# 32-column matmuls in fours over the column quarters, and score pairs over the row halves, in a decoder-layer step

## The chip, the cores and the metric

The kernel runs on one core of a Trainium2 chip. The metric is the time of one execution on the device in microseconds, taken as the median of the runs. The engines are TensorE (PE in the profile; its weight loads are PEld), VectorE (DVE), ScalarE (ACT), GpSimd (POOL) and SyncE (SP), which here only issues transfers.

## What is computed

One layer of a hybrid decoder for two groups with the same weights: a prompt of 1024 tokens, and 8 samples of 4 new tokens each, with 512 past tokens of keys and values in pages of 128. Cut to what the change touches, the reference is:

```python
def diff_attn_core(q, k, v, q_pos, k_pos, lam):
    s = jnp.einsum('bqhid,bkhid->bhiqk', q, k) * (ATTN_HEAD_DIM ** -0.5)   # two maps i, heads h, d = 64
    s = jnp.where(rel >= 0, s + bias, -jnp.inf)
    pr = jax.nn.softmax(s, axis=-1)
    a = pr[:, :, 0] - lam * pr[:, :, 1]
    return jnp.einsum('bhqk,bkhd->bqhd', a, v)                             # v: 128 wide
# prompt: 8 blocks of 128 queries; samples: past_k = cache_k[page_table], 4 heads, 4 pages each
mem_k, mem_v = memory_kv(mem_prompt, p)                                    # the samples have cached ones
s = jnp.einsum('bqhd,bmhd->bhqm', cq, mem_k) * (CA_HEAD_DIM ** -0.5)       # 4 heads of 256, 256 memory tokens
co = jnp.einsum('bhqm,bmhd->bqhd', jax.nn.softmax(s, -1), mem_v)
```

Around it stand an RMS norm and input projection, a diagonal state-space recurrence with its gate, the output projection, and a gated feed-forward of width 2816 with a convolution. All is float32; the large products are made of three matmuls each on a high and a low part (type fp32r).

## The kernel before

The program is one long stream per engine. Stages are written as Python generators that yield costs; `drive` and `par` interleave them by rates and so set the order in which instructions are emitted, and a scheduler then places them engine by engine, by priority and by when their inputs are ready. Each engine runs its own row of instructions strictly in that order. Tiles come from pools with a fixed number of buffers; a tile whose buffer is still in use waits.

In time, the stages are: input projection head by head with the prompt attention of the head before (0 to about 480 us); from about 390 to 646 us the state-space recurrence (`ssm_setup`, `ssm_data`, `ssm_out`), keys and values of the prompt's memory (`memory_kv`) and the samples' attention over their pages; gate and output projection; from 782 us cross-attention (`wq_head`, `ca_head`, `sample_keys`); from 984 us `sample_values` beside the first part of the cross-attention's output projection; from about 1054 us the rest of it and the feed-forward.

Five places matter here.

*Prompt scores* (`attention.score`). For each block of 128 queries and each map i, whose 64 features lie on the lower or upper 64 partitions, chunks of up to 512 keys go through `mm3` (L180 to L182): high x high, low x high, high x low into a tile `S` of one PSUM bank. A DVE reduction adds the bias and keeps the running minimum. The pool `ps_s` has three such tiles; `ps_o` has one bank for the output `ov` of `value`.

*Paged keys* (`sample_attention.keys`). Four samples share a PSUM tile `Sp`, sample b4 in partitions 32 b4 to 32 b4 + 31 (`tile_position=(0, 32 * b4)`). For each sample the four pages are gathered by SP into one of five buffers `pg`, transposed in four (L1381), copied by ACT into `KT`, and after every second page four matmuls of 256 columns (one per head) follow at L1387. All samples' pages go one sample after the other.

*Paged values* (`values`). Sample by sample, page by page: a gather into `pg`, then one matmul of 512 columns (L1433) into the sample's quarter of `Op`; a fifth one takes the new values `vs_`.

*Memory keys* (`sample_keys`). Per head and sample: a load `kt` (three buffers), transposes (L1793), a copy to `KT`, two matmuls of 256 columns into the sample's quarter of `Ssm` (L1799).

*Memory values* (`sample_values`). 32 pieces `vt` of 128 x 512 (seven buffers, loaded by POOL's queue six ahead), each followed by one matmul of 512 columns into a quarter of `Op` (L1870). Of these four places, the first reads:

```python
if pg % 2:
    for h in range(NH):
        nc.tensor.matmul(Sp[rows, 256 * (pg // 2):256 * (pg // 2) + 256], lhsT=Qb[:, h, b, :],
                         rhs=KT[:, h, :], start=h == 0, stop=h == NH - 1,
                         tile_position=(0, 32 * b4))
```

Of the kernel before, what the change touches and what calls it, by code (L numbers as in the profile page):

```python
# [67 lines left out]
def hymba_step(ctx: ExitStack, tc: tile.TileContext, A: dict, O: dict, upto=99, dbg=None):  # L68
# [7 lines left out]
    def par(*streams):  # L76
        # each stream: a generator of costs, its rate, the share it starts behind, its boost
# [109 lines left out]
    class Carve:  # L187
        """Small tiles cut from a few large ones; a tag names one region."""
# [132 lines left out]
    def ssm_params(st, ps):  # L321
# [58 lines left out]
        # cos and sin of the chunk angle times 0..15, and times 0, 16, ..., 112  # L380
# [67 lines left out]
    ps_s = pool(p2, "ps_s", 3, space=PSUM)  # L448
    ps_o = pool(p2, "ps_o", 1, space=PSUM)
# [217 lines left out]
    def attention(h, last):  # L667
# [9 lines left out]
        def score(t):  # L677
# [3 lines left out]
            Pm = []  # L681
# [3 lines left out]
            split(qh, ql, qT[:, 128 * t:128 * t + 128])  # L685
            for i in range(2):
                pr = slice(64 * i, 64 * i + 64)
                P = at.tile([128, SEQ], F32, tag="P", name=f"P{i}", bufs=4)
                init = 3.0e38
                for c0 in range(0, n, 512):  # L690
                    c1 = min(n, c0 + 512)
                    S = ps_s.tile([128, 512], F32, tag="S", name="S")
                    mm3(S[:, :c1 - c0], qh[pr], ql[pr], kh[pr, c0:c1], kl[pr, c0:c1], True, True)
                    b0 = SEQ - n + c0
                    nc.vector.tensor_tensor_reduce(out=P[:, c0:c1], in0=S[:, :c1 - c0], in1=base[:, b0:b0 + c1 - c0],
                                                   scale=-1.0, scalar=init, op0=ALU.add, op1=ALU.min,
                                                   accum_out=mx[:, i:i + 1])
                    init = mx[:, i:i + 1]
                    yield (c1 - c0) * 3 / 2.4
                nc.vector.tensor_scalar(out=mx[:, i:i + 1], in0=mx[:, i:i + 1], scalar1=sl, scalar2=None,  # L700
                                        op0=ALU.mult)
                nc.scalar.activation(out=P[:, :n], in_=P[:, :n], func=AF.Exp, scale=-sl, bias=mx[:, i:i + 1],
                                     accum_out=ssum[:, t, i:i + 1])
                Pm.append(P)
                yield 10
# [23 lines left out]
        def value(t):  # L729
            ov = ps_o.tile([128, 260], F32, tag="ov", name="ov")  # L730
# [375 lines left out]
    # sample group: the recurrence step by step  # L1106
# [77 lines left out]
    # keys and values of the prompt's memory  # L1184
# [78 lines left out]
    # differential attention of the sample group over its pages  # L1263
    sc = {}

    def sample_tables(sa):
# [29 lines left out]
        # columns: the past, new keys for the first four samples, new keys for the last four  # L1296
# [46 lines left out]
    def sample_attention(sa):  # L1343
# [6 lines left out]
        def gather(src, j):  # L1350
            g = sa.tile([128, 512], F32, tag="pg", name="pg", bufs=PGB)
# [17 lines left out]
        def keys(s):  # L1369
            Sp = ps_j.tile([128, PAST], F32, tag="pjb", name="Sp")  # L1370
            Sps.append(Sp)
            for b4 in range(4):
                b = 4 * s + b4
                rows = slice(32 * b4, 32 * b4 + 32)
                for pg in range(NPG):
                    if pg % 2 == 0:
                        KT = sa.tile([128, NH, 256], F32, tag="KT", name="KT", bufs=2)
                    kp_ = gather(kpg, NPG * b + pg)
# [3 lines left out]
                    c = 128 * (pg % 2)  # L1382
                    nc.scalar.copy(KT[:, :, c:c + 128], pt.rearrange("p (h k) -> p h k", h=4))
                    yield 440
                    if pg % 2:
                        for h in range(NH):
                            nc.tensor.matmul(Sp[rows, 256 * (pg // 2):256 * (pg // 2) + 256], lhsT=Qb[:, h, b, :],  # L1387
                                             rhs=KT[:, h, :], start=h == 0, stop=h == NH - 1,
                                             tile_position=(0, 32 * b4))
                        yield 500  # L1390

        def soft(s):
            Sp = Sps[s]
            Pm = sa.tile([128, PAST + NS], F32, tag="Pm", name="Pm")
# [27 lines left out]
        def values(s):  # L1422
# [3 lines left out]
            for b4 in range(4):  # L1426
                b = 4 * s + b4
                for pg in range(NPG + 1):
                    if pg < NPG:
# [681 lines left out]
```

## Time and profile before

| | us |
|---|---|
| median of 3 runs (1910.13 to 1913.94) | 1912.89 |
| span of the profiled execution | 1912.4 |
| TensorE busy in it | 1842.9 (96%) |
| VectorE busy | 1144.4 (60%) |
| ScalarE busy | 623.8 (33%) |
| GpSimd busy | 473.8 (25%) |

The profiled execution's own time is its span, from its first to its last instruction; it lies within 0.5 us of the median. Busy time is the time in which at least one record of an engine runs. Matmuls are pipelined and their records overlap, so what a matmul costs is read from the start of one to the start of the next, or from the length of a group. A line in the profile may be that of a helper: L54 is every DVE and ACT instruction, L180 to L182 every `mm3`. The granted clock (PEclk) is a share of 2.4 GHz.

### The profile page before, as it was taken

The numbers are of one execution on the slowest core, as the hardware profiler recorded it, in microseconds if no ns is written. First come the engines' busy times: TensorE is split into PE (matmuls) and PEld (weight loads), VectorE is DVE, ScalarE is ACT, GpSimd is POOL, SyncE is SP. The second block draws the span as 40 slices with busy tenths as digits, with TensorE's granted clock in tenths as the row PEclk, the third lists the DMA queues.
The fourth block names the chain that finished last, engine by engine and source line by source line (L and its number), as shares of the span: only waits on it lengthen the run. The fifth ranks groups of instructions, "written<-read, shape, count | busy, mean of one in ns | idle before, by whom it ended". The sixth has DMA issues, their size and how long they took to land. (4 is left out here: it accounts for less than half of the span.)

```text
span 1912.4 us, 29088 instructions
## 1 busy us (share of the span) xinstructions
PE 1842.9 (96%) x11105; PEld 1649.2 (86%) x11105; DVE 1144.4 (60%) x2867; ACT 623.8 (33%) x1425; POOL 473.8 (25%) x547
## 2 busy tenths in 40 slices
PE   7899999889899999999989999999999999999998
PEld 6787897767556799888855999999999999999998
DVE  6976448795876554655452665555656646556554
ACT  6654345545243543344441312112102102112112
POOL 4412321360530024100012333223123123223200
PEclk8888998979799999999999999999999999999999
DMA  7202112134355342322243111011111102102102
GB/s 224 68 28 62 44 48 65 48 108 129 113 147 158 117 145 82 95 85 92 78 154 127 56 37 56 27 52 57 45 34 57 55 23 68 45 23 68 45 23 92
DMA packets 160773, 147.15 MB, mean 77 GB/s; under 512 B 14167, under 2 KB 142067, under 8 KB 160634
## 3 DMA queue, kind: packets, MB, share of 16 engines
q1 hardware_dynamic: 135698, 111.03, 19.2%
q0 software_dynamic: 7232, 18.71, 3.2%
q10 hardware_dynamic: 17704, 15.56, 2.4%
q8 instruction: 87, 1.43, 0.3%
q14 instruction: 52, 0.43, 0.1%
HBM read 120.07 MB, written 25.19 MB: 76 GB/s over the span
## 5 line engine op out<-in xcount | busy, mean ns | idle before, releaser
L54 DVE TENSOR_TENSOR xacc<-xacc,pd 128x384 f32<-128x384 f32 (+1 forms) x264 | 134.9, 518 | 168.7 <-PE pd L182 168.7
L54 ACT CAST whi<-raw 128x1024 fp32r<-128x1024 f32 x74 | 77.5, 1049 | 427.9 <-PE pg L181 332.8
L182 PE MATMUL pv<-Xh,wlo 128*128 128x384 f32 (+1 forms) x528 | 171.3, 325 | 0.3 <-DVE wlo L54 0.3
L180 PE MATMUL pv<-Xh,whi 128*128 128x384 f32 (+1 forms) x528 | 171.6, 325 | 0.0
L180 PE MATMUL pd<-ah,dhi 128*128 128x384 f32 (+1 forms) x528 | 171.2, 325 | 0.1
L180 PE MATMUL pg<-Xh,whi 128*128 128x384 f32 (+1 forms) x528 | 171.2, 324 | 0.0
L181 PE MATMUL pv<-Xl,whi 128*128 128x384 f32 (+1 forms) x528 | 171.1, 324 | 0.0
L182 PE MATMUL pd<-ah,dlo 128*128 128x384 f32 (+1 forms) x528 | 170.9, 324 | 0.0
L181 PE MATMUL pd<-al,dhi 128*128 128x384 f32 (+1 forms) x528 | 170.1, 322 | 0.5 <-DVE al L54 0.5
L181 PE MATMUL pg<-Xl,whi 128*128 128x384 f32 (+1 forms) x528 | 170.6, 323 | 0.0
L182 PE MATMUL pg<-Xh,wlo 128*128 128x384 f32 (+1 forms) x528 | 170.2, 322 | 0.0
L54 DVE TENSOR_TENSOR wlo<-raw,whi 128x1024 fp32r<-128x1024 f32 x74 | 107.0, 1448 | 21.1 <-ACT whi L54 20.8
L180 PE MATMUL pp<-Mh,whi 128*128 128x384 f32 (+1 forms) x336 | 109.2, 328 | 0.9 <-ACT Mh L54 0.9
L181 PE MATMUL pp<-Ml,whi 128*128 128x384 f32 (+1 forms) x336 | 108.5, 326 | 0.8 <-DVE Ml L54 0.8
L182 PE MATMUL pp<-Mh,wlo 128*128 128x384 f32 (+1 forms) x336 | 109.2, 327 | 0.0
L798 POOL TENSOR_TENSOR raw<-raw,GT 128x1024 f32<-128x1024 f32 x30 | 67.0, 2233 | 165.2 <-DMA raw<-in_ffn_wg_dram 99.2
L180 PE MATMUL pj<-whi,Xh 128*128 128x384 f32 (+1 forms) x288 | 105.3, 367 | 1.5 <-DVE mx L54 1.5
L181 PE MATMUL pj<-wlo,Xh 128*128 128x384 f32 (+1 forms) x288 | 103.2, 359 | 0.2
L182 PE MATMUL pj<-whi,Xl 128*128 128x384 f32 (+1 forms) x288 | 103.2, 359 | 0.0
L182 PEld LDWEIGHTS pv<-Xh,wlo 128*128 128x128 f32 x528 | 99.7, 189 | 0.5 <-DVE wlo L54 0.4
L181 PEld LDWEIGHTS pd<-al,dhi 128*128 128x128 f32 x528 | 99.2, 188 | 0.8 <-DVE al L54 0.8
L180 PEld LDWEIGHTS pd<-ah,dhi 128*128 128x128 f32 x528 | 99.0, 188 | 0.9 <-ACT ah L54 0.5
(813 smaller groups left out, 4873.8 us busy)
## 6 DMA issues: line engine op xcount, KB each, us to landing
raw<-in_ffn_wg_dram SPq DMA_DIRECT2D x22, 512.0 KB, 3.8
raw<-in_ffn_wv_dram SPq DMA_DIRECT2D x22, 512.0 KB, 3.8
raw<-in_ffn_wd_dram SPq DMA_DIRECT2D x22, 512.0 KB, 3.6
pg<-in_cache_k_dram SPq DMA_DIRECT2D x32, 256.0 KB, 2.7
pg<-in_cache_v_dram SPq DMA_DIRECT2D x32, 256.0 KB, 3.3
kt<-in_cache_mem_k_dram SPq DMA_DIRECT2D x32, 256.0 KB, 2.8
vt<-in_cache_mem_v_dram POOLq DMA_DIRECT2D x32, 256.0 KB, 3.9
raw<-in_w_in_dram SPq DMA_DIRECT2D x48, 128.0 KB, 2.5
```

Source lines behind the costliest of these rows:

```text
L54: return f(*a, **k)
L180: nc.tensor.matmul(out, lhsT=wh, rhs=xh, start=start, stop=False)
L181: nc.tensor.matmul(out, lhsT=wh, rhs=xl, start=False, stop=False)
L182: nc.tensor.matmul(out, lhsT=wl, rhs=xh, start=False, stop=stop)
L798: nc.gpsimd.tensor_tensor(out=raw, in0=raw, in1=g.unsqueeze(2).to_broadcast([128, KD, 128]), op=ALU.mult)
```

## The change

The four 32-column products are reordered so that the matmuls of the four column quarters follow each other (`for b4 in QUADS`, that is 3, 2, 1, 0), under a raised priority that keeps a group together. For this, operands of four samples must be there at once:

- paged keys: page by page over four samples; `KT` holds one page of four samples (8 KB a partition), 16 matmuls of 128 columns follow; page buffers fall from five to two;
- paged values: one tile `V` holds one page of four samples, from four gathers; four matmuls of 512 columns. `KT`, `V` and the probabilities `Pm` share two buffers `big`;
- memory keys: `KT` holds four samples, in one buffer; eight matmuls of 256 columns; loads `kt` have two buffers, `co` two instead of three;
- memory values: 16 pieces of four samples by 256 columns, in three buffers; four matmuls of 256 columns.

The prompt scores take both maps in one tile of two banks, and each of the three matmuls is issued for map 1 and map 0 in turn. `ps_o` is gone: `ps_s` has two tiles of two banks, which also serve the output `ov` and the transposes of x.

```diff
+QUADS = (3, 2, 1, 0)
-    ps_s = pool(p2, "ps_s", 3, space=PSUM)
-    ps_o = pool(p2, "ps_o", 1, space=PSUM)
+    ps_s = pool(p2, "ps_s", 2, space=PSUM)
...
+        pts = ps_s.tile([128, 8, 128], F32, tag="S", name="pt")
         for b in range(2):
-            pt = ps_s.tile([128, 4, 128], F32, tag="S", name="pt")
+            pt = pts[:, 4 * b:4 * b + 4]
...
+                S = ps_s.tile([128, 2, 512], F32, tag="S", name="S")
+                with tc.high_priority():
+                    for j, (q_, k_) in enumerate(((ql, kh), (qh, kl), (qh, kh))):
+                        for i in (1, 0):
+                            pr = slice(64 * i, 64 * i + 64)
+                            nc.tensor.matmul(S[:, i, :w], lhsT=q_[pr], rhs=k_[pr, c0:c1], start=j == 0, stop=j == 2,
+                                             tile_position=(64 * i, 0))
-                    mm3(S[:, :c1 - c0], qh[pr], ql[pr], kh[pr, c0:c1], kl[pr, c0:c1], True, True)
...
-            ov = ps_o.tile([128, 260], F32, tag="ov", name="ov")
+            ov = ps_s.tile([128, 2, 512], F32, tag="S", name="ov")[:, 0]
...
+            for pg in range(NPG):
+                KT = sa.tile([128, 4, NH, 128], F32, tag="big", name="KT", bufs=KTB)
+                for b4 in range(4):
+                    kp_ = gather(kpg, NPG * (4 * s + b4) + pg)
...
+                with tc.high_priority():
+                    for h in range(NH):
+                        for b4 in QUADS:
+                            nc.tensor.matmul(Sp[32 * b4:32 * b4 + 32, 128 * pg:128 * pg + 128],
+                                             lhsT=Qb[:, h, 4 * s + b4, :], rhs=KT[:, b4, h, :],
+                                             start=h == 0, stop=h == NH - 1, tile_position=(0, 32 * b4))
...
+                    V = sa.tile([128, 4, 512], F32, tag="big", name="V", bufs=KTB)
+                    rh = [gather(vpg, NPG * (4 * s + b4) + pg, V[:, b4]) for b4 in range(4)]
...
+                    for b4 in QUADS:
+                        lh = aT[:128 if pg < NPG else NS, pg, 32 * b4:32 * b4 + 32]
+                        nc.tensor.matmul(Op[32 * b4:32 * b4 + 32, :], lhsT=lh, rhs=rh[b4], start=pg == 0,
+                                         stop=pg == NPG, tile_position=(0, 32 * b4))
...
-    PGB = 5
+    PGB, KTB = 2, 2
...
+            for s in range(2):
+                KT = ca.tile([128, 4, 2, NMEM], F32, tag="KT", name="KT", bufs=CKB)
...
+                    for z in range(2):
+                        for b4 in QUADS:
+                            nc.tensor.matmul(Ssm[32 * b4:32 * b4 + 32, :], lhsT=Qc[:, z, 4 * s + b4, :],
...
+                vt = wx.tile([128, 4, 256], F32, tag="vt", name="vt", bufs=3)
...
+                    for b4 in QUADS:
+                        nc.tensor.matmul(Op[32 * b4:32 * b4 + 32, 256 * g:256 * g + 256],
```

(`CKB` is 1.) The scheduler lays out every engine anew. Three places of TensorE's row show what became of it; `pj`, `pp` and `pjm` are projections, `ov` the attention's output, `pt` a transpose, `yp` the recurrence's output.

TensorE, prompt scores of the first heads, before: one map's three matmuls are taken apart, others stand between.

```order
L180 MATMUL ov<-aTh,vh 128x256
L180 MATMUL S<-kh,qh 128x512
L647 MATMUL pt<-ident,qk 128x128 x2
L181 MATMUL S<-kl,qh 128x512
L181 MATMUL ov<-aTl,vh 128x256
```

The same, after: both maps, three times in turn (x2 is map 1 and map 0), in the middle of an output's accumulation.

```order
L181 MATMUL ov<-aTh,vh 128x256
L696 MATMUL S<-kh,ql 128x512 x2
L696 MATMUL S<-kl,qh 128x512 x2
L696 MATMUL S<-kh,qh 128x512 x2
L182 MATMUL ov<-aTl,vh 128x256
```

The six score matmuls moved together; those of the output that stood among them moved behind.

TensorE, the samples' paged values, before: one matmul of one quarter at a time, between the recurrence's matmuls.

```order
L1049 MATMUL yp<-T,Ug 128x128
L1050 MATMUL yp<-CLr,Hr 128x128
L1433 MATMUL Op<-pg,aT 32x512
L965 MATMUL kp<-CLr,Bbr 32x128
L1381 MATMUL pt<-ident,pg 128x128 x4
L1053 MATMUL yp<-CLi,Hi 128x128
L1433 MATMUL Op<-pg,aT 32x512
```

The paged keys near the same place, after: 16 matmuls, four quarters four times, in one piece.

```order
L1054 MATMUL yp<-T,Ug 128x128
L1055 MATMUL yp<-CLr,Hr 128x128
L1058 MATMUL yp<-CLi,Hi 128x128
L1390 MATMUL Sp<-KT,Qb 32x128 x16
L983 MATMUL sp<-ident,T 128x128 x4
```

The paged values stand likewise in ten rows of x4, eight with a page and two with the new values, the keys in eight rows of x16.

TensorE, memory values beside the output projection, before: single matmuls.

```order
L1870 MATMUL Op<-vt,PT 32x512
L182 MATMUL pp<-Mh_11054,wlo 128x384
L180 MATMUL pp<-Mh_11055,whi 128x384
L181 MATMUL pp<-Ml_11058,whi 128x384
L182 MATMUL pp<-Mh_11052,wlo 128x384
L1870 MATMUL Op<-vt,PT 32x512
```

The same, after: fours, with ten to twelve projection matmuls between.

```order
L1882 MATMUL Op<-vt,PT 32x256 x4
L182 MATMUL pp<-col_8554,whi 128x384
L183 MATMUL pp<-coh_8552,wlo 128x384
L182 MATMUL pp<-Ml_11004,whi 128x384
L183 MATMUL pp<-Mh_10998,wlo 128x384
```

Sixteen such fours take the place of the 32 single ones.

## Rows read from the trace of the kernel before

**Rows 1.** Windows: length, busy us (records) of PE, PEld, DVE, ACT, POOL; clock, DMA, GB/s.

```profile
0.00:110.00 110.00, 90.42 (x457) 74.93 (x457) 90.78 (x455) 71.79 (x222) 47.02 (x97) 0.88 0.46 134
110.00:360.00 250.00, 245.71 (x1371) 212.59 (x1371) 149.45 (x553) 121.78 (x397) 52.67 (x76) 0.94 0.16 46
360.00:440.00 80.00, 66.03 (x423) 50.05 (x422) 73.62 (x233) 43.55 (x122) 46.70 (x47) 0.81 0.34 106
440.00:646.00 206.00, 195.67 (x1251) 131.38 (x1250) 135.61 (x320) 79.33 (x150) 46.06 (x40) 0.94 0.45 139
...
782.00:984.00 202.00, 196.60 (x1242) 169.16 (x1240) 108.61 (x434) 88.64 (x213) 5.83 (x6) 0.99 0.26 84
984.00:1054.00 70.00, 67.47 (x244) 34.70 (x245) 20.88 (x44) 14.36 (x32) 21.85 (x37) 0.98 0.49 163
1054.00:1912.00 858.00, 847.81 (x5305) 843.72 (x5305) 490.44 (x678) 147.69 (x180) 217.94 (x214) 1.00 0.16 48
```

**Rows 2.** Windows of L1387 (two), L1433, L1799, L1870 alone, in this order.

```profile
400.00:440.00 40.00, 7.63 (x32) 3.27 (x32) 0.87 0.42 135
440.00:646.00 206.00, 25.90 (x96) 10.59 (x96) 0.94 0.45 139
...
540.00:646.00 106.00, 39.63 (x80) 6.19 (x80) 0.99 0.53 161
...
782.00:984.00 202.00, 32.33 (x128) 11.12 (x128) 0.99 0.26 84
...
984.00:1054.00 70.00, 31.04 (x64) 4.00 (x64) 0.98 0.49 163
```

**Rows 3.** Timeline of TensorE, groups of 32-column matmuls: start, length, line, records.

```profile
1008.95 1.04 PE L1870 MATMUL Op<-vt,PT 128*32 128x512 f32 x2
...
1006.72 1.05 PE L1870 MATMUL Op<-vt,PT 128*32 128x512 f32 x4
...
1014.26 1.06 PE L1870 MATMUL Op<-vt,PT 128*32 128x512 f32 x6
...
820.59 1.05 PE L1799 MATMUL Ssm<-KT,Qc 128*32 128x256 f32 x4
...
429.88 1.91 PE L1387 MATMUL Sp<-KT,Qb 128*32 128x256 f32 x8
```

**Rows 4.** Timeline of TensorE, prompt scores: both maps together, then one alone.

```profile
433.34 0.51 PE L180 MATMUL S<-kh,qh 64*128 64x384 f32 x2
...
433.80 0.52 PE L182 MATMUL S<-kh,ql 64*128 64x384 f32 x2
434.16 0.33 PE L180 MATMUL S<-kh,qh 64*128 64x384 f32 x1
...
434.78 0.66 PE L1381 MATMUL pt<-ident,pg 128*128 128x128 f32 x4
```

**Rows 5.** DMA issues: count, KB each, median us from issue to landing.

```profile
pg<-in_cache_v_dram SPq DMA_DIRECT2D x32, 256.0 KB, 3.3
vt<-in_cache_mem_v_dram POOLq DMA_DIRECT2D x32, 256.0 KB, 3.9
```

**Rows 6.** Waits of POOL: us in total, times, longest.

```profile
POOL vt L1863 <- PE Op L1870: 35.1, 21, 3.6
```

**Rows 7.** Windows of the tile S alone (PE, PEld, DVE, ACT).

```profile
0.00:110.00 110.00, 13.50 (x57) 7.75 (x57) 8.80 (x18) 0.00 (x0) 0.88 0.46 134
...
110.00:360.00 250.00, 44.02 (x160) 23.91 (x159) 32.06 (x55) 0.00 (x0) 0.94 0.16 46
...
360.00:470.00 110.00, 18.61 (x72) 11.44 (x72) 13.39 (x24) 0.00 (x0) 0.86 0.35 109
```

**Rows 8.** Timeline of TensorE: first and last matmul of one attention output.

```profile
442.88 0.38 PE L180 MATMUL ov<-aTh,vh 128*128 128x256 f32 x1 [0.71 <-ACT aTh L54]
...
449.79 0.28 PE L182 MATMUL ov<-aTh,vl 128*128 128x128 f32 x1
```

**Rows 9.** Window of 20 us in which VectorE leads.

```profile
500.00:520.00 20.00, 17.47 (x74) 11.40 (x74) 17.18 (x33) 3.12 (x6) 12.37 (x12) 0.57 0.13 41
```

More of the change, by code (lines that the diff above doesn't have):

```diff
@@ L685, in score @@
             split(qh, ql, qT[:, 128 * t:128 * t + 128])
-            for i in range(2):
[L687 to L692, printed above, removed]
-                    mm3(S[:, :c1 - c0], qh[pr], ql[pr], kh[pr, c0:c1], kl[pr, c0:c1], True, True)
[L694 to L699, printed above, removed]
+            Pm = [at.tile([128, SEQ], F32, tag="P", name=f"P{i}", bufs=4) for i in range(2)]
@@ new lines, in score @@
+            for c0 in range(0, n, 512):
+                c1 = min(n, c0 + 512)
+                w = c1 - c0
+                S = ps_s.tile([128, 2, 512], F32, tag="S", name="S")
[5 more added lines that the diff above has]
+                                             tile_position=(64 * i, 0))
+                yield w * 3 / 2.4
+                b0 = SEQ - n + c0
+                for i in range(2):
+                    nc.vector.tensor_tensor_reduce(out=Pm[i][:, c0:c1], in0=S[:, i, :w], in1=base[:, b0:b0 + w],
+                                                   scale=-1.0, scalar=3.0e38 if c0 == 0 else mx[:, i:i + 1],
+                                                   op0=ALU.add, op1=ALU.min, accum_out=mx[:, i:i + 1])
+                yield w * 3 / 2.4
@@ L1381, in keys @@
                         nc.tensor.transpose(pt[:, 128 * h:128 * h + 128], kp_[:, 128 * h:128 * h + 128], ident)
-                    c = 128 * (pg % 2)
-                    nc.scalar.copy(KT[:, :, c:c + 128], pt.rearrange("p (h k) -> p h k", h=4))
+                    nc.scalar.copy(KT[:, b4], pt.rearrange("p (h k) -> p h k", h=4))
                     yield 440
[L1385 to L1390, printed above, removed]
+                with tc.high_priority():
[4 more added lines that the diff above has]
+                                             start=h == 0, stop=h == NH - 1, tile_position=(0, 32 * b4))
+                yield 1000
         def soft(s):
             Sp = Sps[s]
-            Pm = sa.tile([128, PAST + NS], F32, tag="Pm", name="Pm")
+            Pm = sa.tile([128, PAST + NS], F32, tag="big", name="Pm", bufs=KTB)
             mx = sa.tile([128, 1], F32, tag="mxs", name="mxs")
@@ L1425, in values @@
             Op = ps_x.tile([128, 512], F32, tag="x", name="Op")
[L1426 to L1429, printed above, removed]
[L1430 to L1435 removed]
+            for pg in range(NPG + 1):
+                if pg < NPG:
+                    V = sa.tile([128, 4, 512], F32, tag="big", name="V", bufs=KTB)
+                    rh = [gather(vpg, NPG * (4 * s + b4) + pg, V[:, b4]) for b4 in range(4)]
+                else:
+                    rh = [vs_] * 4
+                yield 10
+                with tc.high_priority():
+                    for b4 in QUADS:
+                        lh = aT[:128 if pg < NPG else NS, pg, 32 * b4:32 * b4 + 32]
+                        nc.tensor.matmul(Op[32 * b4:32 * b4 + 32, :], lhsT=lh, rhs=rh[b4], start=pg == 0,
+                                         stop=pg == NPG, tile_position=(0, 32 * b4))
+                yield 950
             os_ = gp.tile([128, 128], F32, tag="os_", name="os_")
@@ L1777, in ca_head @@
                         continue
[L1778 removed]
+                    co = ca.tile([128, 384], F32, tag="co", name="co", bufs=2)
                     nc.scalar.copy(co[:, :nq], po[:, :nq])
```

79 lines of the change are left out of this document (31 added, 48 removed).

## The prediction

> **What bounds the kernel now.** I read first the busy time of each engine by stage [rows 1]. From 110 us on, TensorE is busy nearly all the time in every stage: 245.7 of 250 us, 195.7 of 206, 196.6 of 202, 67.5 of 70, 847.8 of 858. The exceptions are the first 110 us, where VectorE (DVE) has 90.8 us beside TensorE's 90.4, and 360 to 440 us, where DVE has 73.6 of 80 and TensorE 66.0. So TensorE work that goes is worth most where it is alone at the limit (110 to 360, 782 to 984, 984 to 1054), something where DVE is close behind (440 to 646, 135.6 of 206), and little in the two stretches in which DVE leads. After 1054 us the diff touches nothing.
>
> Next I read what the four groups of 32-column matmuls cost [rows 2]: 33.5 us for the scores against the paged keys (L1387; 7.6 of it ahead of 440 us, 25.9 behind), 39.6 for the paged values (L1433), 32.3 for the memory keys (L1799), 31.0 for the memory values (L1870). Together 136.5 us, 7% of the span, for four small products. The counts are records: each float32 matmul of these lines leaves two.
>
> Then I looked for the thing that the change wants, in the kernel before [rows 3]. Its L1870 matmuls stand in single order among others, but in a few places two or three of different quarters meet. One matmul (2 records) takes 1.04 us, two that meet (4 records) 1.05, three (6 records) 1.06. Four records of one quarter, as in L1799, take 1.05 at half the columns, and eight of one quarter (L1387) 1.91: those follow each other. So matmuls of different column quarters run side by side for 0.01 us each, in this kernel, on this very operation, and those of one quarter do not.
>
> **The change, part by part.** *Sample group.* The work is regrouped, not reduced: 64, 40, 64 and 32 matmuls become 128 of half the columns, 40, 64, and 64 of half the columns, in 8, 10, 8 and 16 groups in which the four quarters alternate. What a group costs is what one quarter's share costs. A paged-key group has per quarter 8 records of 128 columns, as many columns as the x4 row of L1799 at 256: 1.05 us. A paged-value group has 2 records of 512 per quarter: 1.06. A memory-key group has 4 of 256: 1.05 to 1.06. A memory-value group has 2 of 256, half of the 1.06 and no more than all of it: I take 0.6. That is 8 x 1.05 + 10 x 1.06 + 8 x 1.06 + 16 x 0.6 = 8.4 + 10.6 + 8.5 + 9.6 = 37 us for 136.5, so 99 us less TensorE time: 25 at the paged keys, 29 at the values, 24 and 21 at the two memory stages. Four quarters at once are not in these rows (three are). If the fourth had to wait for a second round, each group would cost double, 74 us instead of 37, and the gain would be 62.
> The Trainium skill ("TensorE: Matmul & The Clock Gate", Part 3, Measured speedup vs the span model) speaks against the full figure: it gives 2.38 times for three column tiles and 3.07 for four row tiles. The three-quarter row here gives 3 x 1.04 / 1.06 = 2.94. By the Trainium skill's 3.07 the groups would cost 136.5 / 3.07 = 44 us, an estimate, and the forecast below would be some 5 us later.
>
> *How much of the 99 us reaches the end.* 782 to 984 us: 24 us out of 196.6 busy, DVE at 108.6 and ACT at 88.6 of 202. Nothing else is near its limit, so I take 20. The key tile is now filled for four samples by ACT and has one buffer, and its loads have two instead of three; the 4 us that I leave out are for that. 984 to 1054 us: 21 us out of 67.5. The loads of these values have 0.49 of the DMA engines' time over 70 us; in 49 us the same bytes need 0.70, so they fit, but each lands 3.9 us after its issue [rows 5], and POOL already waits 35.1 us for matmuls to free a buffer [rows 6]. Those waits shrink with the matmuls. From now on three pieces of 512 KB are under way instead of six of 256, so the bytes ahead are the same. POOL issues 16 loads for 32; should each cost four times as much for its four times as many pieces, POOL's 21.9 us in this stage would still be under the 49. I take 16 of 21.
> 440 to 646 us: 19.6 us of the key groups (three quarters of 25.9) and 29 of the values: 48 off 195.7, which leaves 148 against DVE's 135.6. Two engines that both need about 140 of a 158 us stretch do not mesh perfectly, and the new waits are here: two 8 KB buffers serve key tiles, value tiles and probabilities, the page buffers fall from five to two, and a value tile must have all four pages landed (3.3 us from issue to landing [rows 5]) before its group starts. SP issues these pages in order, and behind a page that waits for a buffer stand the memory weights, the recurrence's inputs and its tables. I take two thirds, 32 us. Taken away wholly, this cover costs the 32.
>
> *Prompt scores.* Per chunk, three matmuls of one map and three of the other now alternate between the lower and upper 64 rows. The kernel before has them by accident [rows 4]: three of one map at 384 columns and three of the other at 512 (the x2 rows) run from 433.34 to 434.16, 0.82 us; the three of 384 alone that follow take 434.16 to 434.78, 0.62. Side by side they cost what the longer triple costs. All scores take 13.5 + 44.0 + 18.6 = 76 us of TensorE in the three stretches [rows 7]; halved, 38 saved, less what already pairs. In 0 to 110 and from 360 on DVE sets the pace and I count nothing (at most 7 + 9). In 110 to 360 half is 22 at most; some pairs exist already, and DVE still reads every score. I take 12. The price is the PSUM: three one-bank tiles for scores and one for the output become two tiles of two banks for scores, output and the transposes of x. While an output accumulates, one two-bank tile is left for scores. An output holds its tile long: first matmul at 442.88, last at 449.79 [rows 8]. Bounds for this part: +22 and, with the holds exposed, a loss (last rival).
>
> Sum: 20 + 16 + 32 + 12 = 80 us. The profiled execution's span is 1912.4 us, the median 1912.9, so the two need no correction: **1833 us**.
>
> **Rivals.** *All of it arrives*: 24 + 21 + 48 + 22 and some 5 of the DVE-led stretches, 120 us: about 1793. For it: TensorE is busy above 94% in each of these stages. Against it: the order of each engine is laid out ahead, and DVE is close in 440 to 646.
> *The early part gives nothing*: DVE, POOL and the chain of the recurrence set the length of everything up to 646 us, and only 8 us of the 48 and the two memory stages (36) remain: 1868. For it: DVE at 90.8 of 110 and 73.6 of 80, and from 500 to 520 us DVE is busy 17.2 of 20 while the granted clock is 0.57, mostly the lower of its two levels, 1.2 GHz [rows 9], so TensorE there is not the limit; less work could bring more such stretches. Against it: 245.7 of 250 busy. The Trainium skill names this ("TensorEngine Tiling (Array Packing)", PSUM Bottleneck): tiling speeds up the matmuls, not the emptying of PSUM. The trace agrees so far as the DVE reads of the scores keep their count and size.
> *The shared PSUM tiles turn the sign*: there are 16 outputs in four heads; with 449.79 - 442.88 = 7 us of hold each, 112 us in which the scores have one tile. If the dense matmuls cannot fill it (the second head's memory is freed only when the first head is done), a hold costs up to 6 us, 96 in all, against 68 from the other three terms: 1912 + 96 - 68 = 1940. It decides from 68 / 16 = 4.2 us per output. Against it: TensorE was busy 245.7 of 250 us while the same outputs were held [rows 1], since projections stand between.
> *No side by side at four quarters or for alternated rows*: then only the number of visits falls, and the time is within 4 us of 1912. What meets by accident speaks against it [rows 3, 4].
>
> **How the numbers follow.** Forecast case 0.50 (1812 to 1853); all of it 0.20 (1785 to 1812); early part gives nothing 0.22 (1853 to 1890); turned sign 0.05; no effect 0.03. The range 1793 to 1876 holds the first, some seven tenths of the second and six tenths of the third: 0.50 + 0.15 + 0.14, 0.8. Faster by over 0.2% (about what a measurement of this kernel can tell from no change): 0.92; within: 0.03; slower: 0.05.
>
> **What would show it.** In the profile after: groups of the paged keys at about 1.05 us with 32 records, paged values 1.06 with 8, memory keys 1.06 with 16, memory values about 0.6 with 8, together under 45 us busy instead of 136.5; a triple of score pairs at 512 columns no longer than 0.9 us. The stretch from the first memory query to the end of the memory values, 272 us before, near 236. The time at which the gate's matmuls begin, 646 us before, near 602. Wrong would be: groups at twice these lengths (the fourth quarter waits), TensorE waiting for value pages or for a score tile by tens of us, half-clock stretches beyond those of before, or loads of the memory values landing later than the group that needs them.

## The result, and the profile after

The changed kernel takes 1857.0 us (median of 4 runs, 1851.8 to 1858.4) where the kernel before took 1912.5: a ratio of 0.9711, 95% interval 0.9692 to 0.9730. That is 55 us less, where 80 were forecast (1833 us); the time lies inside the range. The profiled execution has a span of 1854.8 us, 57.6 less than before.

Windows of the kernel after, by its own stages (columns as in [rows 1]: length, busy us of PE, PEld, DVE, ACT, POOL; granted clock, DMA share, GB/s):

```profile
0.00:110.00 110.00, 85.11 (x454) 72.11 (x454) 85.17 (x447) 69.07 (x211) 48.57 (x97) 0.88 0.47 134
110.00:352.00 242.00, 226.94 (x1403) 205.71 (x1403) 156.75 (x577) 125.52 (x421) 54.69 (x77) 0.95 0.17 49
352.00:430.00 78.00, 55.13 (x444) 45.78 (x443) 64.05 (x212) 39.59 (x107) 48.39 (x47) 0.74 0.36 110
430.00:618.00 188.00, 156.26 (x1330) 124.25 (x1328) 148.56 (x343) 81.18 (x157) 45.07 (x39) 0.89 0.51 156
755.00:940.00 185.00, 175.89 (x1227) 164.23 (x1226) 110.06 (x429) 86.87 (x208) 5.37 (x5) 0.96 0.31 93
940.00:994.00 54.00, 49.18 (x316) 35.59 (x315) 23.71 (x49) 15.44 (x36) 16.10 (x20) 0.91 0.69 211
994.00:1854.00 860.00, 850.14 (x5309) 845.75 (x5307) 482.70 (x677) 148.02 (x181) 223.49 (x215) 0.99 0.16 48
```

Against [rows 1] the reader is to see two things. First, TensorE has room in the stages that the change touches: 156 of 188 us where it had been 196 of 206, 49 of 54 where it had been 67 of 70. Second, the clock is lower there: 0.89 for 0.94, 0.96 for 0.99, 0.91 for 0.98. The gate begins at 618 us (646 before), the first memory query is at 755 (782), the last memory-value group ends at 993 (1054). So 28 us were won ahead of the gate, 34 from the first memory query to the end of the memory values (272 to 238), and about 4 were lost elsewhere.

The groups themselves, in the timeline of TensorE after (start, length, line, records; L1390 paged keys, L1439 paged values, L1809 memory keys, L1882 memory values, L696 prompt scores):

```profile
394.27 1.08 PE L1390 MATMUL Sp<-KT,Qb 128*32 128x128 f32 x32
...
543.86 1.07 PE L1439 MATMUL Op<-V,aT 128*32 128x512 f32 x8
...
788.88 1.07 PE L1809 MATMUL Ssm<-KT,Qc 128*32 128x256 f32 x16
...
955.35 0.64 PE L1882 MATMUL Op<-vt,PT 128*32 128x256 f32 x8
...
125.62 0.50 PE L696 MATMUL S<-kh,ql 64*128 64x512 f32 x2
125.96 0.39 PE L696 MATMUL S<-kl,qh 64*128 64x512 f32 x2
126.19 0.39 PE L696 MATMUL S<-kh,qh 64*128 64x512 f32 x2
...
502.19 1.86 PE L1390 MATMUL Sp<-KT,Qb 128*32 128x128 f32 x32
...
603.68 1.93 PE L1439 MATMUL Op<-vs__78,aT 32*32 32x512 f32 x8
```

All four quarters run side by side, at 1.08, 1.07, 1.07 and 0.64 us where 1.05, 1.06, 1.06 and 0.6 were forecast. A pair of score triples at 512 columns takes 0.96 us (125.62 to 126.58), a little over the 0.9 that the prediction named as the limit. The last two rows are groups in stretches at the lower clock.

Groups of instructions of the kernel after, TensorE alone (count, busy us and mean ns, idle time ahead of them and its releaser):

```profile
L1882 PE MATMUL Op<-vt,PT 128*32 128x256 f32 x128 | 10.9, 416 | 2.7 <-DMA vt<-in_cache_mem_v_dram 2.7
L1390 PE MATMUL Sp<-KT,Qb 128*32 128x128 f32 x256 | 9.4, 292 | 1.2 <-ACT KT L55 1.2
L1439 PE MATMUL Op<-V,aT 128*32 128x512 f32 x64 | 8.9, 629 | 2.8 <-DMA V<-in_cache_v_dram 2.8
L1809 PE MATMUL Ssm<-KT,Qc 128*32 128x256 f32 x128 | 8.6, 384 | 2.1 <-ACT KT L55 2.1
L1439 PE MATMUL Op<-vs__78,aT 32*32 32x512 f32 x16 | 3.0, 828 | 0.0
```

Together 40.8 us, for 136.5 in [rows 2]: 96 us less, where 99 were forecast. The waits for loads ahead of these matmuls are 2.7 and 2.8 us, and the transposes ahead of the paged keys (L1384) wait 7.8 us for their pages, 6.1 of it at 412 us. So the work went as forecast; most of what failed to arrive has to be looked for outside these lines.

### The profile page after: what moved, and what is told of

It reads as the page before. It is cut to its first block, busy times and chain, and to the rows that moved or that the text cites. A ratio compares the mean times of both kernels' runs of the same rounds, so it can differ in the third digit from the quotient of the medians.

```text
span 1854.8 us, 29387 instructions
## 1 busy us (share of the span) xinstructions
PE 1732.8 (93%) x11297; PEld 1627.2 (88%) x11297; DVE 1142.1 (62%) x2867; ACT 620.6 (33%) x1425; POOL 477.4 (26%) x531
## 4 chain that ended last, share of the span: by engine, by line
PE 79%; DVE 10%; ACT 3%; DMA 2%; issue 1%; POOL 0%; SPq 0%; ACTq 0%; DVEq 0%; POOLq 0%
PE pp L181 5%; PE pp L182 5%; PE pp L183 5%; PE pv L183 5%; PE pv L181 5%; PE pv L182 5%; PE pd L183 5%; PE pd L182 5%; PE pd L181 5%; PE pg L181 4%; PE pg L182 4%; PE pg L183 4%; PE pj L181 2%; PE pj L182 2%; PE pj L183 2%
## 5 line engine op out<-in xcount | busy, mean ns | idle before, releaser
L181 PEld LDWEIGHTS pv<-Xh,whi 128*128 128x128 f32 x528 | 99.9, 189 | 0.0
```

The source lines that it names most:

```text
L181: nc.tensor.matmul(out, lhsT=wh, rhs=xh, start=start, stop=False)
```

## The experiments

Each row gives the median, the ratio to the kernel before with its 95% interval, and from the timeline of the profiled execution the end of the last attention head (the last matmul that spreads its scale, tile bc), the first matmul of the gate (tile zp), and the time between.

| kernel | us | ratio (interval) | attention ends | gate begins | between |
|---|---|---|---|---|---|
| before | 1912.5 | 1 | 483 | 646 | 163 |
| after | 1857.0 | 0.9711 (0.9692-0.9730) | 475 | 618 | 143 |
| scores_only | 1918.2 | 1.0032 (1.0013-1.0051) | 488 | 646 | 158 |
| memory_only | 1879.3 | 0.9814 (0.9777-0.9850) | 482 | 645 | 163 |
| sample_only | 1869.3 | 0.9780 (0.9754-0.9806) | 487 | 630 | 143 |
| keys_in_turn | 1852.5 | 0.9698 (0.9664-0.9731) | 476 | 614 | 138 |
| maps_in_turn | 1848.9 | 0.9684 (0.9655-0.9713) | 468 | 605 | 136 |
| x_three | 1860.2 | 0.9734 (0.9704-0.9764) | 476 | 619 | 143 |
| cost_true | 1848.4 | 0.9676 (0.9647-0.9705) | 464 | 607 | 142 |
| dve_less | 1861.7 | 0.9743 (0.9714-0.9773) | 479 | 624 | 145 |
| no_pages | 1856.3 | 0.9701 (0.9678-0.9724) | 475 | 614 | 138 |
| pm_own | 1853.3 | 0.9693 (0.9674-0.9712) | 474 | 611 | 137 |
| best1 | 1856.5 | 0.9713 (0.9692-0.9734) | 466 | 613 | 148 |
| hp_both | 1850.9 | 0.9700 (0.9674-0.9725) | 474 | 614 | 140 |

The changed kernel and its seven variants that compute the same (keys_in_turn, maps_in_turn, x_three, cost_true, pm_own, best1, hp_both) lie within 12 us of one another, and each interval overlaps that of the changed kernel. Differences below some 6 us are therefore read from the traces, not from the times. The traces are one execution each: a kernel whose order is laid out anew can shift by as much for reasons that its edit does not name.

**The parts alone: scores_only, memory_only, sample_only.** The first is the kernel before with the score part, the second with the memory keys and values, the third the changed kernel with the scores as before.

```
scores_only:  + S = ps_s.tile([128, 2, 512]), both maps per chunk, ov and x transposes from ps_s
memory_only:  + sample_keys and sample_values in fours
sample_only:  memory_only + keys(s), values(s) in fours, buffers of 8 KB shared
```

> The kernel before with the prompt-score part alone: maps in pairs, score, output and x transposes in two two-bank tiles. In the trace of the changed kernel the dense projections end 13 us earlier (365 to 352). Theory (the parts add up by stage): those 13 us are this part's and reach the end less what the start loses, so 1900 to 1904. Rival (the early part is paced by DVE and the recurrence, so the scores alone bring nothing that lasts): the projections end near 352 but the gate's matmuls still begin within 3 us of 646, and the time is 1909 to 1914. Second rival (the shared tiles cost what the pairs bring): the projections end at 360 or later and the time is 1912 or more.

> The kernel before with the memory keys and memory values alone in fours. In the changed kernel the stretch from the first memory query to the end of the memory values took 239 us for 272. Theory: those 33 us reach the end whole, since nothing behind them waits for DVE: 1878 to 1882. By my forecast's terms (20 and 16) 1877. Rival (part of the 33 us is owed to the earlier stages, for instance loads that found the queues emptier): 1885 or more.

> The changed kernel with the prompt scores as before: only the sample group's matmuls go in fours. Theory (the parts add up): 1857 plus the 9 to 13 us of the scores, 1866 to 1870, with the gate's matmuls beginning near 630. Rival (the score part brings nothing that lasts, the early gain is the paged keys' and values' alone): 1855 to 1860, the gate's matmuls near 618. If the shared score tiles cost more than the pairs bring: below 1855.

Measured: memory alone 33 us off, as expected from the stage. The paged keys and values bring 10 more (1879.3 to 1869.3; the two intervals overlap, and in the profiled executions the gate begins 15 us earlier). The scores bring 12 beside the sample part (1869.3 to 1857.0) and cost 6 alone: slower, with an interval that excludes 1. So the parts do not add up, and the first expectation missed: 1918 lies above its 1900 to 1904 and above its rival's 1909 to 1914 too. Which part is credited with what hangs on the order in which they are added: put in first, the scores cost 6 and the paged keys and values bring 28 (1918.2 - 1857.0, less the 33 of the memory part). Without an order it can only be said that the two bring 22 together (1879.3 to 1857.0). In scores_only the score matmuls are as short as in the changed kernel, 40.0 us busy against 76.1:

```profile
0.00:620.00 620.00, 40.02 (x288) 23.52 (x288) 52.11 (x96) 0.00 (x0) 0.91 0.33 97
```

(window of the tile S of scores_only; PE first, DVE third). Its dense projections end at 355 us (365 before), but the last attention at 488 (483): 15 us are given back between, and the gate begins at 646 all the same. That much is the rival named for it: early gain that does not last. The profiled execution loses its 4 us behind the gate's first matmul: the last paged-value group ends at 654 us (641 before), among the gate's matmuls, and the first memory query comes at 785 (782).

**keys_in_turn and maps_in_turn.** The matmuls of a group, reordered.

```
-  for h in range(NH):                 -  for j, (q_, k_) in enumerate(...):
-      for b4 in QUADS:                -      for i in (1, 0):
+  for b4 in QUADS:                    +  for i in (1, 0):
+      for h in range(NH):             +      for j, (q_, k_) in enumerate(...):
```

> The changed kernel, its groups, buffers and loads as they are, but in the groups of the paged keys and of the memory keys each quarter's matmuls stand together, quarter after quarter, instead of in alternation. Theory (matmuls of different quarters run side by side only where they stand next to each other): the two lines, 9.4 and 8.6 us busy, go back to near 30 and 30 us, the memory-key stage grows by 12 to 22 us, the early part by 0 to 16: 1870 to 1893. Rival (the gain is from fewer visits and fewer waits between them, not from running side by side): both lines stay under 15 us and the time within 4 us of 1857.

> The changed kernel, its score tiles and loads as they are, but the three matmuls of one map stand together, then the three of the other. Theory (as with the memory keys, a matmul need not stand right beside the one that it runs with: those of the second map start while the first map's still run): the score tile's busy time stays at 40 to 55 us in the first 618 us, and the time at 1852 to 1862. Rival (row halves run together only in alternation): the busy time goes back towards the 76 us of before, and the time to the 1866 to 1872 of the kernel without the score part.

Timeline of TensorE of keys_in_turn, paged keys and memory keys:

```profile
392.76 2.46 PE L1390 MATMUL Sp<-KT,Qb 128*32 128x128 f32 x32
...
784.55 1.09 PE L1809 MATMUL Ssm<-KT,Qc 128*32 128x256 f32 x16
```

The memory keys, four records of each quarter, take 1.09 us without alternation and 1.07 with it; one quarter's four alone take 1.05 [rows 3], so four quarters in turn would be 4.2. The paged keys, eight records of each quarter, take 2.46 instead of 1.08, still well under four times that. In that group the next quarter starts 0.47 us after the one ahead, with its fifth record. So with four records of 256 columns a quarter's matmuls need not stand beside those that they run with, and with eight of 128 it costs more than double; nothing between was run. The theory was wrong for one line and half right for the other. maps_in_turn kept its theory's busy time (44.1 us for the score tile, 40 to 55 expected) and came out faster than either reading, 1848.9. Its trace shows another order than the one in which the matmuls are issued:

```profile
126.76 0.50 PE L696 MATMUL S<-kh,ql 64*128 64x512 f32 x2
127.10 0.40 PE L696 MATMUL S<-kl,qh 64*128 64x512 f32 x2
127.33 0.40 PE L696 MATMUL S<-kh,qh 64*128 64x512 f32 x2
```

The program issues (kh,ql), (kl,qh), (kh,qh) of one map and then of the other; the records start in pairs, one of each map, 0.97 us for all six. More important for the time: keys_in_turn has 10 us more TensorE work in the paged keys (19.7 us busy for 9.4) and is no slower. **Ahead of the gate, TensorE work added in one place did not move the end.** It does not follow that TensorE has no part in it: the granted clock rose with the work (0.960 for 0.951), so that TensorE's busy time over the whole kernel is the same, 1732.4 us for 1732.8.

**x_three and cost_true: what the score part cost ahead of the last attention.**

```
x_three:    pt = third half tile from ps_t, the others from ps_s, one half each
cost_true:  -  yield w * 3 / 2.4      (the second of two per pair of chunks)
            +  yield 10
```

> The changed kernel with the transposes of x in three half tiles in turn (two of the score tiles, one of the bank that later serves the transposed probabilities), as many as before, instead of two whole tiles of two halves. In the changed kernel the last transposes of x are at 71 us (57 before) and the first scores at 64 (57). Theory (the shared tiles hold the start back, and behind it TensorE is the limit): last transposes before 60 us, first scores near 57, the dense projections end 5 to 7 us earlier and the time is 1849 to 1854. Rival (the start is paced by DVE, 85 of 110 us, and the lag is caught up by itself): 1854 to 1860.

> The changed kernel with one number of the planner changed: a pair of score chunks is charged to its stream as the length of one triple, as it now runs, not of two. Theory (the stream of the attention, charged twice, is set back behind the others, and the recurrence on DVE can only start when it has ended): the last attention ends 5 to 12 us earlier than 475 us, the gate's matmuls begin that much ahead of 618, time 1845 to 1852. Rival (the attention's own chain of scores, exponentials, transposes and values sets its end): within 4 us of 1857. A loss, 1861 or more, if the dense projections, which then come later, set the early part.

x_three does away with the late start. Timeline of TensorE, last transposes of x and first scores:

```profile
55.96 0.43 PE L520 MATMUL pt<-ident,xt 32*128 32x32 f32 x4
56.76 0.50 PE L698 MATMUL S<-kh,ql 64*128 64x128 f32 x4 [0.38 <-ACT kh L55]
```

In the changed kernel these transposes stand at 70.35 us. Yet the last attention ends at 476 and the gate begins at 619, as without it: the rival held, the shared tiles' 14 us at the start cost nothing. cost_true came out as its theory said: attention ends 11 us earlier, the gate begins 11.5 earlier, 1848.4 us. The planner had charged a pair of chunks twice over; that this set the attention back behind the other streams fits, but is not shown by it alone. Its interval still touches that of the changed kernel, so the gain of 8.6 us is likely, not certain. And maps_in_turn, which changes no cost, has the attention end 7 us earlier, the gate begin 13 earlier, and about the same time (1848.9): a new order of the instructions moves as much by itself. These two are the fastest kernels measured here.

**dve_less, no_pages, pm_own, hp_both: what holds the stage between attention and gate.** Windows of that stage, before and after:

```profile
483.00:646.00 163.00, 153.99 (x921) 96.34 (x919) 114.10 (x250) 56.28 (x102) 43.13 (x37) 0.93 0.47 144
```

```profile
475.00:618.00 143.00, 114.71 (x925) 86.77 (x924) 121.04 (x252) 54.15 (x100) 42.06 (x35) 0.85 0.54 166
```

TensorE was the limit (154 of 163) and is not any more (115 of 143); DVE has 121. Of the 39 us that TensorE is busy less, 20 went off the stage and 19 became idle time of TensorE (28 us for 9). Four kernels take away one suspect each:

```
dve_less:  - cmul(nc.vector, Hr, Hi, vr, vi, Rr, Ri, va, vb)   + two copies on ACT
no_pages:  - V tile and its four page loads                    + rh = [tabS[:, 0:512]] * 4
pm_own:    Pm in a tag of its own instead of "big"; xs and oj in the places of others
hp_both:   both starting-state transposes into one PSUM tile, one DVE copy
```

> The changed kernel without the last complex product of the recurrence on DVE: six operations of 128x512 for each of four quarters are left out, and ACT copies the scanned states instead (the recurrence's results are not computed). DVE loses 24 operations that follow each other at 0.61 us, 14.6 us, and is 121 us busy of the 143 between the last attention and the gate. Theory (after the last attention DVE is the limit, not TensorE, and this is why the paged keys and values brought 16 to 20 us and not 32): the gate's matmuls begin at 604 to 610 us instead of 618, time 1843 to 1849. Rival (the loads of the pages, the two shared buffers or the half clock of TensorE set this stage): within 4 us of 1857.

> The changed kernel without the loads of the 32 value pages: the paged-value groups multiply a table that lies in SBUF anyway (the sample attention's result is not computed), so they wait for no load and hold none of the two shared 8 KB buffers. In the changed kernel the last four value groups come 4 to 9 us after one another, load, group, load, and the last stands at 604 us, 14 us ahead of the gate; with DVE's load cut by 18 us the gate did not come earlier and the value groups ended at 623. Theory (the loads of the value pages behind two shared buffers end the stage): the gate's matmuls begin 8 to 16 us ahead of 618, time 1841 to 1849. Rival (the chain of the recurrence, DVE, ACT and TensorE by turns at half its clock, ends the stage just as late): within 4 us of 1857.

> The changed kernel with a buffer of its own for the probabilities over the pages, so that only key tiles and value tiles share the two of 8 KB (two small scratch tiles share others' places to make room). In the changed kernel the second value tile of the second half waits 10 us for the transposes of these probabilities, from 576 to 586 us. Theory (this hold delays the last value groups and they end the stage): the last value group is at 593 to 598 instead of 604, the gate begins 4 to 10 us earlier, time 1847 to 1853. Rival (loads or recurrence end the stage as late without the hold): within 4 us of 1857.

> The changed kernel with one edit in the sample group's recurrence: the two transposes of its starting state go into one PSUM tile and one DVE copy reads both, where the second transpose had to wait for the copy of the first. In the changed kernel that transpose waits 11.5 us at the front of TensorE's queue, 486 to 497.5 us, with page transposes, recurrence matmuls and memory projections behind it; the copy that it waits for stands on DVE behind scans and copies that take three to seven times their usual time while POOL runs. Leaving out DVE work, or the value pages, did not shorten the stage. Theory (freed TensorE time is lost in such in-order waits, since TensorE no longer has a backlog): the 11.5 us wait goes, and the gate's matmuls begin 4 to 11 us ahead of 618, time 1846 to 1853. Rival (the recurrence's own chain, DVE beside POOL, sets the stage, and TensorE waits somewhere else instead): within 4 us of 1857.

Windows of the stage in dve_less, then in no_pages:

```profile
478.00:624.00 146.00, 125.70 (x931) 95.33 (x930) 102.70 (x215) 60.45 (x110) 40.51 (x35) 0.79 0.52 163
```

```profile
475.00:614.00 139.00, 114.64 (x910) 91.91 (x909) 118.24 (x253) 56.98 (x104) 41.60 (x35) 0.84 0.38 111
```

With 18 us of DVE work gone the stage is as long, and the time rather longer: my theory that DVE's load alone is the limit fell. Two things went the other way in that run: the granted clock of the stage was 0.79 for 0.85, and TensorE was busy for 126 us instead of 115. In dve_less the value groups came last, waiting for their pages:

```profile
609.97 1.94 PE L1440 MATMUL Op<-V,aT 128*32 128x512 f32 x8 [5.13 <-DMA V<-in_cache_v_dram]
619.33 3.44 PE L1440 MATMUL Op<-V,aT 128*32 128x512 f32 x16
622.70 1.06 PE L1440 MATMUL Op<-vs__78,aT 32*32 32x512 f32 x8
623.69 0.45 PE L181 MATMUL zp<-Mh,whi 128*128 128x384 f32 x1
```

But with all 32 value loads gone the gate begins only 4.6 us earlier and the time stays (1856.3): that theory fell too. The chain of work that the profile follows back from the end shows what stands in for what was taken away. Two pieces of it near the end of the stage in the kernel after, then one in dve_less and one in no_pages (start, length, what):

```profile
596.50 5.74 DMA V<-in_cache_v_dram
602.28 3.33 PE Op L1439 x16
```

```profile
604.29 5.63 DMA V<-in_cache_v_dram
```

```profile
596.44 4.74 DMA raw<-in_w_out_dram
```

Without the value pages, a load of the output projection's weights stands at the same time. Added up over the stage, this chain has 69 us of DVE, 46 of TensorE and 10 of loads in the kernel after; 43, 60 and 23 in dve_less; 51, 56 and 6 in no_pages; 28, 86 and 9 in keys_in_turn. Less DVE work did make DVE's part shorter, and TensorE and loads took its place. (What releases what is inferred from semaphores, so these sums are a reading, not a measurement.)

The hold on the shared 8 KB buffer (pm_own) is worth 7 us at the gate, the last value group starts at 592 us instead of 604, and the time is 1853.3, within noise of both readings. hp_both removes the longest wait of TensorE and gets another in its place. Waits of TensorE in the kernel after:

```profile
PE hp L1118 <- DVE h L55: 11.5, 1, 11.5
PE pt L518 <- ACT scr L55: 8.3, 2, 5.3
PE pt L1384 <- DMA pg<-in_cache_k_dram: 7.8, 2, 6.1
```

and in hp_both:

```profile
PE bp L1129 <- DVE h L55: 10.1, 1, 10.1
```

The next instruction in TensorE's queue, a transpose into the same bank (bp), now waits for the same DVE copy. The gate came 3.6 us earlier, where 4 to 11 were expected; the wait is 1.4 us shorter and the attention ended 1 us sooner. The time, 1850.9, lies in the range of the theory, but the wait that the theory was about has only moved.

**best1** takes three edits together.

```
best1 = cost_true + maps_in_turn + pm_own
```

> The changed kernel with three edits together: the pair of score chunks charged as one triple, the maps' triples one after the other, the probabilities in a buffer of their own. Alone the first two came out at 1848 and 1849 for 1857. If their gains are from different places (the order of the streams ahead of the last attention, the score tile's release) and add: 1836 to 1843. If both only shift the same order of the streams: 1845 to 1851.

Neither: 1856.5. The attention ends 9 us earlier, about as in cost_true, but the sample group has been set back in turn. Timeline of TensorE in best1:

```profile
611.17 1.92 PE L1439 MATMUL Op<-V,aT 128*32 128x512 f32 x16
613.24 0.44 PE L181 MATMUL zp<-Mh,whi 128*128 128x384 f32 x1
```

Its paged-value groups run past the gate's start (the last ends at 626 us), where they ended at 606 in the changed kernel. That alone is not what the three edits lose against cost_true: there the last group ends at 625 us, and the kernel is 8 us faster. Between attention and gate best1 needs 148 us where cost_true needs 142, and why stays open.

## Why the prediction was right, and where its sum was not

The time lies in the range, but 24 us above the forecast, and by the bands of the prediction it is not in that of the forecast case (1812 to 1853) but 4 us into that of "the early part gives nothing" (1853 to 1890). Of the signs named, the groups' lengths and the stretch of the memory stages came (238 us for 236 forecast); the gate did not (618 for 602).

*The work removed: right.* 40.8 us for the groups where 37 were forecast; the fourth quarter runs with the others. The excess is mostly clock: groups of 1.86 and 1.93 us stand where it is at its lower level. The estimate of 44 us from the Trainium skill ("TensorE: Matmul & The Clock Gate", Part 3, Measured speedup vs the span model) is about as far off the 40.8 as the rows were (3 us and 4 us). At the lengths of the groups that run at full clock the sum is 8 x 1.08 + 10 x 1.06 + 8 x 1.07 + 16 x 0.64 = 38 us, near the rows' 37; four quarters give 4 x 1.05 / 1.07 = 3.9 times for the memory keys.

*Memory keys and values, 20 + 16: right.* 33 us alone, 34 in the changed kernel. By stage it is 16 for the keys (first memory query to last key group, 200.1 to 184.6 us) and 18 for the values. TensorE was alone at its limit there, and what it lost in work it gave in time.

*Paged keys and values, 32: the term that failed.* Put in ahead of the scores, they bring 10 us by time, 15 by the profiled gate; beside the scores 28 by time. Without an order: this term and the scores' 12 brought 22 of 44 together, and all that is missing from the 80 but some 3 us is missing there. The step was "I take two thirds" of 48. It took DVE's 135.6 of 206 as the next limit and left room above it for waits. The runs show that the part before 483 us gave nothing (the attention's end moves from 482 to 487 us between memory_only and sample_only), and that the stage behind it shrinks by 20 and then stays at 136 to 148 us, whatever is taken away: 18 us of DVE work, 32 loads, a buffer's hold, the longest wait of TensorE. My reading is that before, a full TensorE covered all of these, and that now each of them is exposed in turn; the idle time of TensorE in this stage, 9 us before and 28 after, fits that.

*Prompt scores, 12: right in size by luck.* The 12 us exist only beside the sample part; alone the part costs 6, the sign of the rival of the shared PSUM tiles. But no row shows that rival's mechanism: TensorE waits 2.6 us for score tiles in scores_only (on DVE's mx) and 2.1 in the changed kernel, where it waited 8.7 before; the late start costs nothing; and the loss of scores_only lies behind the gate. What moved the attention's end in the changed kernel is the planner's charge (11 us), and also the order of the maps (7 us). Whether the same charge makes scores_only slower was not run.

*"Early part gives nothing", 1868:* nearer by time (11 us off) than the forecast (24 off), though its account is too strong: 28 of the 44 us forecast ahead of the gate came, where it allowed 8. The sign it named, more half-clock stretches, is there: the mean granted clock of the stage between attention and gate falls from 0.93 to 0.85, that of the whole from 0.966 to 0.951. Window of the kernel after in which the longest wait lies:

```profile
480.00:500.00 20.00, 6.57 (x51) 5.11 (x52) 19.93 (x33) 1.76 (x3) 14.29 (x13) 0.67 0.30 95
```

TensorE is busy 6.57 of 20 us, 11.5 of the rest in the wait on hp above, and the granted clock falls to 0.67 on average, most of the time its lower level of 1.2 GHz; the paged-key group that follows at 502 us takes 1.86 us instead of 1.08. So this wait was paid twice. Over the kernel the touched lines lost 132 us (96 and 36 of the scores), TensorE's busy time 110, the span 58.

*The rest:* the stages that the change does not touch came out 4 us longer, 3 of them behind the memory values, which the forecast had at nothing. No run shows why.

**What stays open** is what holds the stage between attention and gate at some 140 us. In the changed kernel no engine is busy for more than 0.85 of it. In seven of the kernels (after, keys_in_turn, x_three, cost_true, no_pages, pm_own, hp_both) the recurrence's last matmuls end as the gate's first begins, as they did before the change; in dve_less, best1 and maps_in_turn a value group stands between. That several chains of nearly the same length run through all engines is my reading. The sums of the profile's chain above, which shift from DVE to TensorE and loads at nearly the same length, fit it; no run shows it outright. The lower clock was not tried apart from the rest: TensorE has its lower level for some 43 of the 143 us, 23 of 163 before (from the mean clocks 0.85 and 0.93).

## What to carry to other kernels

Small matmuls on different column quarters or row halves ran side by side here when they were near each other in program order: without alternation at four records of a quarter, at more than twice the length at eight. What such a change was worth is nearly the time forecast only in the stages in which TensorE was alone at its limit (33 of 36 us); where another engine was busy for two thirds of the stage, the regrouping gave 10 to 15 of 48 us by itself, and with the scores 22 of 44. So look first at what the full TensorE has been covering, and add up parts only after running them in both orders. When matmuls become cheaper, look again at the costs by which a planner orders the streams: here one number of them went with an attention that ended 11 us earlier, and did not add to the other edits.

## What the runs showed of the hardware

**Matmuls pass one another.** In maps_in_turn and keys_in_turn matmuls start ahead of others that stand before them in the program, if these wait for their own quarter or half. The Trainium skill ("TensorE: Matmul & The Clock Gate", Part 3, The mechanism) says that matmuls start and end strictly in program order. The rows differ: in that order the memory keys' group, whose four matmul records of a quarter follow each other 0.2 us apart, could not end in 1.09 us. (The trace holds no program order; that the engine had the order of the edit is seen from the paged keys, which the same edit makes 2.46 us long.) The measurement decides.

**DVE instructions last several times longer while POOL computes.** Timeline of DVE in the kernel after:

```profile
481.46 1.36 DVE L55 TENSOR_TENSOR_SCAN vr<-rho,vr 128x128 f32<-128x128 f32 x4
482.73 1.07 DVE L55 TENSOR_SCALAR rs_t<-vk 128x2 int32<-128x2 int32 x1
...
485.36 4.14 DVE L55 TENSOR_TENSOR_SCAN vi<-rho,vi 128x128 f32<-128x128 f32 x4
...
491.96 3.68 DVE L55 COPY uz<-uTs 32x128 f32<-32x128 f32 x4
...
497.04 0.15 DVE L55 SCALAR_TENSOR_TENSOR rs_t<-rs_t,vk 128x2 f32<-128x2 f32 x1
```

and of POOL:

```profile
482.42 1.36 POOL L956 TENSOR_TENSOR q<-nCi,Lr 128x576 f32<-128x576 f32 x1
483.74 1.68 POOL L957 TENSOR_TENSOR q<-Cr,Li 128x576 f32<-128x576 f32 x1
...
495.52 1.06 POOL L216 TENSOR_TENSOR q<-Es,Es 128x512 f32<-128x512 f32 x1
```

Two columns take 1.07 us instead of 0.15, about one POOL operation; four scans 4.14 instead of 1.36. It ends with the last operation of that row of POOL's, at 496.6 us. The Trainium skill ("SBUF — State Buffer", SBUF: two separate sides) describes such a thing: a port pair that POOL and certain DVE instructions (two-port modes, or two inputs in SBUF) hold as a lock, each for a whole instruction. The lengths agree; which of the slowed instructions meet that condition, no row shows. By these lengths DVE, which counts as busy in these 14 us (19.9 of 20 in that slice), mostly waits, and the copy that TensorE's 11.5 us wait hung on stands behind them, at 497.11. The same slowing is in the trace before (a 128x2 operation of 1.41 us at 485 us), where TensorE had other work. So "DVE 121 of 143" was in part such waiting; taking POOL's work away was not tried.
